# The MLP's second product by Strassen's algorithm, in seven passes over all inner features

## The chip, the cores and the metric

The kernel runs on one core of a Trainium2 chip. The metric is the device time in microseconds (us) of one execution; the time of a kernel is the median of several runs.

## The reference

A trunk of two layers over 1024 tokens of 1024 features, in float32. Each layer is a mixer with its residual and then an MLP with its residual; the mixer of layer 0 is two groups of heads ("ab"), that of layer 1 a latent attention ("MLA"). A last norm ends it. The change is in the MLP's second product:

```
for layer in range(DEPTH):
    x = x + (ab_mixer if layer % 2 == 0 else mla_mixer)(rms_norm(x, ...))
    hf = rms_norm(x, ffn_norm[layer])
    x = x + jnp.square(jax.nn.relu(hf @ ffn_w1[layer])) @ ffn_w2[layer]
return rms_norm(x, final_norm)
```

`ffn_w1` is 1024 x 4096 and `ffn_w2` 4096 x 1024.

## The kernel before

Activations lie with features on partitions: eight tiles x[m] of 128 features by 1024 tokens. To keep float32 precision each operand is split in a high and a low half of TensorE's faster type (`split`, L350, for activations, `fetch`, L255, for weights: ScalarE casts the high half, VectorE or POOL subtracts for the low one), and every product is three: high by high, high by low, low by high. Weight tiles of 512 KB come through SP's DMA queue in the order of a list written by `plan` (L230).

**First product** (`strassen_up`, L566). It goes by Strassen's algorithm in Winograd's form: 16 quads of two hidden tiles, seven products each, 12 matmuls of 128x512 a product. The order on TensorE, VectorE and ScalarE is as the code is written (a manual schedule). While product g runs, VectorE and ScalarE make the halves of the weights of product g + 3, from sums that VectorE forms (L143), and take results out of PSUM (L615 to L630). The finished hidden tiles, after relu, norm and square, go to DRAM (hd).

**Second product** (`ffn`, L446). Blocks fb of four hidden tiles; for each, four weight tiles; for each of these two output tiles; for each a `gemm` (L284) of 4 hidden tiles x 3 x 2 token halves = 24 matmuls of 128x512. So 8 x 4 x 2 x 24 = 1536 matmuls a layer. After each gemm VectorE adds 128x1024 from PSUM to x[m] (L486). The hidden tiles of the next block are loaded and split during a block (L360, L361). In layer 0 the last block calls `finish` (`next_norm`, L693) for each tile as it is done: halves for MLA, its square added to ss by VectorE (L373), and the tile stored. In layer 1 the last block goes by token pieces of 512, 256 and 256 (`f2_pieces`, L512), and `tail` (L778) does the final norm for each piece: squares, sums over features on TensorE (L381), an inverse root in a dozen small VectorE operations (L333), a spread to all partitions (L433, L435), and eight multiplications with stores (L799, L800), six on VectorE and two on POOL, stores by SP's and ScalarE's queues.

After layer 0 MLA begins with two tiles of its input projection (`latent`, L1345), 48 matmuls each, and after the tenth step of six matmuls the sums over ss (`x_col`).

Of the kernel before, what the change touches and what calls it, by code (L numbers as in the profile page):

```python
# [17 lines left out]
P = 128  # L18
D = 1024
# [4 lines left out]
FB = 8  # L24
FT = 4
# [64 lines left out]
NQ = FB * FT // 2  # L90
H5 = 512

# [80 lines left out]

class Kern:
# [55 lines left out]
    def plan(self):  # L230
        A = self.A
        w = [(A["w_g"], NK * 48, True)]
# [12 lines left out]
        self.wready = deque()  # L245

    def ffn_plan(self, layer):

        out = [None, None]
        for i in range(FB):  # L250
            for j in range(NK // 2):
                out.append((self.A["w2"][layer, i, j], 1024, layer == 1 and i == FB - 1))
        return out
# [30 lines left out]
    def gemm(self, ps, hi, lo, off, step, xh, xl, m=P, cols=FULL, ks=None):  # L284
        nc = self.nc
        n = len(xh)
        for k in range(n) if ks is None else ks:
            wh = hi[:, off + k * step:off + k * step + m]
            wl = lo[:, off + k * step:off + k * step + m]
            for i, (w, x) in enumerate(((wh, xh[k]), (wh, xl[k]), (wl, xh[k]))):  # L290
                for o, t, c in cols:
                    nc.tensor.matmul(ps[:m, o:o + c], lhsT=w, rhs=x[:, t:t + c],  # L292
                                     start=k == 0 and i == 0, stop=k == n - 1 and i == 2)
# [84 lines left out]
    def rstd_sums(self, ps, ss, nt=NC):  # L378
# [4 lines left out]
        self.drop(ss)  # L383
# [17 lines left out]
    def rstd_col(self, ss, n, name, mul=None, nt=NC):  # L401
        ps = self.bank()
        self.rstd_sums(ps, ss, nt)
        return self.rstd_from(ps, n, name, mul, nt)
# [41 lines left out]
    def ffn(self, layer, X, ss, spill, finish, pieces=None):  # L446
        nc = self.nc
        self.lo_engine = nc.vector
        hd = [self.dp.tile([P, T], F32, name=f"hd{layer}_{i}") for i in range(FB * FT)]
        hs = {}  # L450

        def load(i, t=None):
            if t is None:
                t = self.slot(name="h")
                nc.sync.dma_start(out=t, in_=hd[i])
            hs[i] = self.split(t)
            self.drop(t)

        self.strassen_up(layer, X, ss, hd, load)
        with ExitStack() as st:  # L460
            self.pairs_of_banks()
            p2 = st.enter_context(self.tc.tile_pool(name=f"pf{layer}", bufs=2, space=PSUM, reuse_waits="tile"))
            self.bank = lambda: self.pm.tile([P, 512], F32, tag="mm", name=self.uid("bank"))
            turn = [0]

            def ps_tile():
                n = turn[0]
                turn[0] += 1
                if n % 2 == 0:
                    return self.mm()  # L470
                return p2.tile([P, T], F32, tag="mm2", name=self.uid("mmb"))

            x = []

            def operands(fb):
                return [hs[fb * FT + i][0] for i in range(FT)], [hs[fb * FT + i][1] for i in range(FT)]

            def f2(fb):
                hh, hl = operands(fb)
                for mp in range(NK // 2):  # L480
                    hi, lo = self.weights()
                    for j in range(2):
                        m = 2 * mp + j
                        ps = ps_tile()
                        self.gemm(ps, hi, lo, j * 512, P, hh, hl)
                        nc.vector.tensor_tensor(out=x[m], in0=x[m], in1=ps, op=ALU.add)  # L486
                        if fb == FB - 1:
                            finish(x, m)
                    self.release()


            def f2_pieces(fb):
                hh, hl = operands(fb)
                w = []
                with self.tc.manual_schedule(engines={mybir.EngineType.PE}):
                    for pi, (t, n) in enumerate(pieces):
                        cols = slice(t, t + n)
                        for ms in ([0, 1, 2, 3], [4], [5], [6], [7]) if pi == 0 else [[m] for m in range(NK)]:

                            ps = {}  # L500
                            for ks in (range(FT - 1), (FT - 1,)):
                                for m in ms:
                                    if pi == 0 and m % 2 == 0 and ks[0] == 0:
                                        w.append(self.weights())
                                        if m < 4:
                                            self.fetch()
                                    if ks[0] == 0:
                                        ps[m] = ps_tile()
                                    self.gemm(ps[m], *w[m // 2], (m % 2) * 512, P, hh, hl, cols=((0, t, n),), ks=ks)
                            for m in ms:  # L510
                                with self.tc.high_priority():
                                    nc.vector.tensor_tensor(out=x[m][:, cols], in0=x[m][:, cols],  # L512
                                                            in1=ps[m][:, :n], op=ALU.add)
                                finish(x, m, pi)
                    self.flush()
                for p in w:
                    self.drop(*p)

            for m in range(NK):
                t = self.slot(name="x")  # L520
                nc.sync.dma_start(out=t, in_=spill[m])
                x.append(t)
            for fb in range(FB):
                if fb + 1 < FB:
                    for i in range((fb + 1) * FT, (fb + 2) * FT):
                        load(i)
                if fb == FB - 1 and pieces:
                    f2_pieces(fb)
                else:
                    f2(fb)  # L530
                for k in range(FT):
                    self.drop(*hs.pop(fb * FT + k))
# [33 lines left out]
    def strassen_up(self, layer, X, ss, hd, load):  # L566
# [10 lines left out]
        ht = deque()  # L577
# [61 lines left out]
        def square(q, i):  # L639
            c = quads[q].pop(f"c{i}")  # L640
            nc.scalar.activation(c, c, AF.Square)
            nc.sync.dma_start(out=hd[2 * q + i], in_=c)
            self.drop(c)

        with tc.manual_schedule(engines={mybir.EngineType.PE, mybir.EngineType.DVE, mybir.EngineType.Activation}):
            up.load(1)

            for g in range(4):
                product(g, range(NK // 2 - 1), last=False)
            for g in range(N):  # L650
# [5 lines left out]
                if g == 3:  # L656
                    ps = self.bank()
                    self.rstd_sums(ps, ss["ss"])
                if g == 6:
# [17 lines left out]
                if q == NQ - 1:  # L677
                    if s == 1:
                        for i in range(FT):
                            t = self.slot(name="h")  # L680
                            nc.sync.dma_start(out=t, in_=hd[i])
                            ht.append(t)
                    if 2 <= s <= 5:
                        load(s - 2, ht.popleft())
                    if s == 5:
                        self.fetch()
                evacuate(g)
            square(NQ - 1, 1)
            self.fetch()
        self.drop(rb[0])  # L690


    def next_norm(self, goff, xh, xl, state, spill):  # L693
        def finish(x, m):
            hi, lo = self.split(x[m], g=self.cst[:, goff + m:goff + m + 1])
            xh.append(hi)
            xl.append(lo)
            state["ss"] = self.sq_add(state.get("ss"), x[m])
# [40 lines left out]
    def run(self):  # L739
# [32 lines left out]
        nh, nl, st = [], [], {}  # L772
        self.ffn(0, X, s, spill[0], self.next_norm(C_CN, nh, nl, st, spill[1]))
        X, s = self.mla(nh, nl, st["ss"], spill[1], spill[2])
        self.tail(X, s, spill[2])


    def tail(self, X, s, spill):  # L778
        nc = self.nc
        pieces = ((0, 512), (512, 256), (768, 256))  # L780
        ss = [None] * len(pieces)
        rc = {}

        def finish(x, m, pi):
            t, n = pieces[pi]
            cols = slice(t, t + n)
            ss[pi] = self.sq_add(ss[pi], x[m][:, cols], n)
            nc.scalar.activation(x[m][:, cols], x[m][:, cols], AF.Copy, scale=self.cst[:, C_FIN + m:C_FIN + m + 1])
            if m < NK - 1:
                return  # L790

            def col():
                rc[pi] = self.rstd_col(ss[pi], D, f"rf{pi}", nt=n // P)

            def norm():
                rb = self.spread(rc[pi], nt=n // P, parts=False)
                for k in range(NK):
                    eng = nc.gpsimd if k % 4 == 3 else nc.vector
                    eng.tensor_tensor(out=x[k][:, cols], in0=x[k][:, cols], in1=rb[:, :n], op=ALU.mult)  # L799
                    (nc.sync if k % 2 == 0 else nc.scalar).dma_start(out=self.out[k][:, cols], in_=x[k][:, cols])  # L800
                self.drop(rb)
            self.later(10, col)
            self.later(14, norm)
        self.ffn(1, X, s, spill, finish, pieces=pieces)
# [978 lines left out]
```

## Time and profile before

| | |
|---|---|
| median of 3 runs | 2547.54 us (2546.87 to 2549.79) |
| the profiled execution | 2546.84 us, its span 2544.8 us |
| first MLP, first product | 470 to 792 us |
| first MLP, second product | 792 to 1147 us |
| second MLP, first product | 1880 to 2169 us |
| second MLP, second product | 2169 to 2526 us |
| TensorE / VectorE / ScalarE / POOL busy | 98% / 64% / 42% / 20% of the span |

The span goes from the first to the last instruction of one execution that the profiler recorded. A group's row gives engine, operation, output and inputs, shape and count, then its busy time and the mean of one in ns, and after the second bar the idle time of the engine before it with what ended that.

### The profile page before, as it was taken

How to read it: one execution, taken by the hardware profiler on the slowest of the kernel's cores; microseconds unless marked ns; L12 is line 12 of the kernel's file. 1: busy time of each engine (PE TensorE's matmuls, PEld its weight loads, DVE VectorE, ACT ScalarE, POOL GpSimd, SP SyncE). 2: the span in 40 equal slices, each digit the busy share in tenths (PEclk: the TensorE clock that was granted, in tenths of full speed). 3: DMA queues.
4: the chain of work that ended last, by engine and by line, in shares of the span. 5: the costliest groups of instructions: out<-in, count | busy, mean ns of one | idle time of the engine just before them, and what ended most of it. 6: DMA issues, size and time to landing. Idle time of an engine off the chain costs nothing.

```text
span 2544.8 us, 31331 instructions
## 1 busy us (share of the span) xinstructions
PE 2482.7 (98%) x12235; PEld 2060.7 (81%) x12235; DVE 1625.9 (64%) x2372; ACT 1066.7 (42%) x1629; POOL 520.1 (20%) x333
## 2 busy tenths in 40 slices
PE   7999989999999999999999999999999999999997
PEld 5788877788888888888788888887878888888886
DVE  6765487766667443354788888886776666634336
ACT  3354444433334111034567777776533333411113
POOL 3233244100000000003445454545300000000001
PEclk9999999999999999999999999999999999999999
DMA  3112123332336322131000000012332334622111
GB/s 113 67 58 73 36 65 107 115 116 91 123 126 248 115 76 75 50 124 51 25 18 22 18 22 17 21 51 75 129 116 99 115 110 157 231 83 99 56 53 67
DMA packets 63091, 217.20 MB, mean 85 GB/s; under 512 B 7168, under 2 KB 10176, under 8 KB 62944
## 3 DMA queue, kind: packets, MB, share of 16 engines
q1 hardware_dynamic: 60608, 210.96, 23.4%
q10 hardware_dynamic: 2304, 4.20, 0.4%
q8 instruction: 97, 1.59, 0.3%
q14 instruction: 50, 0.41, 0.1%
q0 software_dynamic: 32, 0.05, 0.0%
HBM read 160.81 MB, written 54.36 MB: 85 GB/s over the span
## 4 chain that ended last, share of the span: by engine, by line
PE 90%; DVE 7%; issue 1%; ACT 1%; DMA 0%; POOL 0%; DVEq 0%; ACTq 0%; POOLq 0%
PE mm L292 31%; PE mmb L292 14%; PE A L594 7%; PE C L594 7%; PE D L594 7%; PE s L1532 6%; PE po L1585 4%; PE pt L1566 4%; PE pj L292 4%; PE B L594 3%; DVE mx L1536 1%; PE mm L307 1%; PE intra L1213 1%; DVE nm L1538 0%; PE int L1202 0%
## 5 line engine op out<-in xcount | busy, mean ns | idle before, releaser
L292 PE MATMUL mm<-hi,wlo 128*128 128x512 f32 x1160 | 367.1, 396 | 2.6 <-POOL wlo L272 2.5
L292 PE MATMUL mm<-lo,whi 128*128 128x512 f32 x1160 | 367.7, 396 | 0.0
L292 PE MATMUL mm<-hi,whi 128*128 128x512 f32 x1160 | 367.5, 396 | 0.0
L271 ACT CAST whi<-raw 128x1024 fp32r<-128x1024 f32 (+1 forms) x117 | 121.0, 1034 | 436.4 <-PE mmb L292 318.8
L292 PEld LDWEIGHTS mm<-hi,wlo 128*128 128x128 f32 x1160 | 217.9, 189 | 52.6 <-POOL wlo L272 3.0
L292 PEld LDWEIGHTS mm<-lo,whi 128*128 128x128 f32 x1160 | 218.3, 189 | 49.0
L292 PEld LDWEIGHTS mm<-hi,whi 128*128 128x128 f32 x1160 | 218.3, 189 | 48.9 <-issue 0.6
L1551 POOL TENSOR_SCALAR pr<-pr,rs 128x1024 f32<-128x1024 f32 x128 | 143.8, 1124 | 237.9 <-DVE rs L1550 195.9
L594 PE MATMUL A<-xo,wo 128*128 128x512 f32 x768 | 190.9, 397 | 1.4 <-DVE x L719 1.4
L272 POOL TENSOR_TENSOR wlo<-raw,whi 128x1024 fp32r<-128x1024 f32 (+1 forms) x53 | 131.2, 2476 | 290.7 <-ACT whi L271 275.2
L594 PE MATMUL C<-xo,wo 128*128 128x512 f32 x768 | 188.5, 393 | 0.0
L594 PE MATMUL D<-xo,wo 128*128 128x512 f32 x768 | 188.1, 393 | 0.0
L1536 DVE TENSOR_REDUCE mx<-s 128x1 f32<-128x1024 f32 x128 | 155.6, 1215 | 44.8 <-PE s L1532 43.9
L486 DVE TENSOR_TENSOR x<-x,mmb 128x1024 f32<-128x1024 f32 x60 | 73.2, 1219 | 170.9 <-PE mmb L292 170.9
L1544 ACT ACTIVATE pr<-s,nm,rqs 128x1024 f32<-128x1024 f32 x128 | 154.6, 1208 | 52.0 <-DVE nm L1538 48.7
L594 PEld LDWEIGHTS A<-xo,wo 128*128 128x128 f32 x768 | 146.2, 191 | 35.4 <-issue 1.8
L594 PEld LDWEIGHTS C<-xo,wo 128*128 128x128 f32 x768 | 144.1, 188 | 33.7
L594 PEld LDWEIGHTS D<-xo,wo 128*128 128x128 f32 x768 | 144.2, 188 | 33.4
L1568 ACT CAST pth<-pt 128x512 fp32r<-128x512 f32 x256 | 138.0, 589 | 77.0 <-PE pt L1566 76.4
L1570 DVE TENSOR_TENSOR ptl<-pt,pth 128x512 fp32r<-128x512 f32 x256 | 163.7, 680 | 7.1 <-ACT pth L1568 6.2
L486 DVE TENSOR_TENSOR x<-x,mm 128x1024 f32<-128x1024 f32 x60 | 73.2, 1219 | 136.5 <-PE mm L292 136.5
L292 PE MATMUL mmb<-lo,whi 128*128 128x512 f32 x480 | 149.8, 393 | 0.0
(336 smaller groups left out, 4769.0 us busy)
## 6 DMA issues: line engine op xcount, KB each, us to landing
raw<-w SPq DMA_DIRECT2D x128, 512.0 KB, 3.3
hd<-c SPq DMA_DIRECT2D x64, 512.0 KB, 2.6
h<-hd SPq DMA_DIRECT2D x64, 512.0 KB, 4.6
raw<-w_in SPq DMA_DIRECT2D x24, 512.0 KB, 3.2
xs<-x SPq DMA_DIRECT2D x24, 512.0 KB, 2.6
x<-xs SPq DMA_DIRECT2D x24, 512.0 KB, 5.1
x<-xT SPq DMA_DIRECT2D x12, 512.0 KB, 6.3
Dm<-nMd SPq DMA_DIRECT2D x8, 512.0 KB, 3.4
```

The lines of the kernel that those rows point to most:

```text
L271: nc.scalar.copy(out=hi[:, :cols], in_=raw[:, :cols])
L272: self.lo_engine.tensor_tensor(out=lo[:, :cols], in0=raw[:, :cols], in1=f(hi[:, :cols]), op=ALU.subtract)
L292: nc.tensor.matmul(ps[:m, o:o + c], lhsT=w, rhs=x[:, t:t + c], start=k == 0 and i == 0, stop=k == n - 1 and i == 2)
L486: nc.vector.tensor_tensor(out=x[m], in0=x[m], in1=ps, op=ALU.add)
L594: nc.tensor.matmul(ps, lhsT=a, rhs=x, start=first and kk == 0 and j == 0, stop=last and kk == NK // 2 - 1 and j == 2, skip_group_check=not ...
L1532: nc.tensor.matmul(ps[:, hsl], lhsT=lhs[:, qs], rhs=rhs[:, hsl], start=a, stop=z)
L1536: nc.vector.reduce_max(out=mx, in_=ps, axis=AX.X)
L1544: nc.scalar.activation(pr, ps, AF.Exp, bias=nm, scale=r["qs"][:, qb:qb + 1], accum_out=su)
L1551: nc.gpsimd.tensor_scalar(out=pr, in0=pr, scalar1=rs, scalar2=1.0, op0=ALU.mult, op1=ALU.mult)
L1566: nc.tensor.transpose(pt[:, j * P:(j + 1) * P], pr[:, c * P:(c + 1) * P], self.ident)
L1568: nc.scalar.copy(out=pth[half][:, :, qo], in_=pvs[half])
L1570: nc.vector.tensor_tensor(out=ptl[half][:, :, qo], in0=pv, in1=f(pth[half][:, :, qo]), op=ALU.subtract)
```

## The change

The second product goes by Strassen's algorithm too (`strassen_down`). The output's two halves of features by two halves of tokens are the four blocks; inner features are cut in eight blocks kp. Seven passes, in the order `DOWN`, each go over all eight kp, so a pass is 8 steps of 24 matmuls of 128x512, 56 steps and 1344 matmuls a layer. The four PSUM banks of a pass collect over all eight steps, and some over two passes, and are added to x only afterwards, 40 additions of 128x512 a layer (L773), one or two a step during the next pass.

- Weights: three of the seven operands are quarters of w2, the other four are sums of quarters. The sums are made once per layer during the first product (`DownSums`, L240): for every kp four loads, four VectorE operations of 128x1024, four stores to a DRAM tensor sd. In the second product each step fetches and splits one 512 KB weight tile (56 a layer, 32 before).
- Hidden features: `DownInputs` loads quarters of 128 x (2 x 512) with rows of 2 KB, two tiles at a time, in four of the seven passes, four steps ahead; combines two quarters with one VectorE operation in four passes, three steps ahead (L199); and splits one a step, two steps ahead (56 a layer, 32 before).
- Layer 0's end: tiles 4 to 7 of x are finished during the last pass, tiles 0 to 3 after it. The squares are added to ss by POOL. MLA's first two tiles start with input tiles 4 to 7 of both, and go on with 0 to 3.
- Layer 1's end (`Tail`): tokens 512 to 1023 are complete after the last pass but one. Their squares are added by POOL in pass 4, steps 0 to 3, their sums and spread come in steps 5 and 6, and in step 7 POOL multiplies eight tiles of 128x512, each followed by a store in SP's queue. The last pass is done for tokens 0 to 255 first, with weights and inputs kept, then for 256 to 511 tile pair by tile pair; the last piece is multiplied by VectorE (six) and POOL (two).

VectorE in the second product of layer 0. Before, lo is the low half of a hidden tile h, wlo that of a weight tile, x<-x,mm the addition from PSUM:

```order
L361 TENSOR_TENSOR lo_6758<-h_6755,hi_6757 128x1024
L486 TENSOR_TENSOR x_5965<-x_5965,mm_6261 128x1024
L486 TENSOR_TENSOR x_5967<-x_5967,mmb_6287 128x1024
L272 TENSOR_TENSOR wlo_6315<-raw_6313,whi_6314 128x1024
L486 TENSOR_TENSOR x_5969<-x_5969,mm_6319 128x1024
L486 TENSOR_TENSOR x_5971<-x_5971,mmb_6345 128x1024
```

The same engine after the change, two steps of the pass that follows pass 5; hq is a hidden quarter, z a bank of pass 5:

```order
L773 TENSOR_TENSOR x_6109<-x_6109,z_6390 128x512
L773 TENSOR_TENSOR x_6111<-x_6111,z_6390 128x512
L199 TENSOR_TENSOR hq_6003<-hq_6681,hq_6003 128x1024
L412 TENSOR_TENSOR wlo_6729<-raw_6727,whi_6728 128x1024
L502 TENSOR_TENSOR lo_6760<-hq_6003,hi_6759 128x1024
L773 TENSOR_TENSOR x_6149<-x_6149,z_6391 128x512
L773 TENSOR_TENSOR x_6151<-x_6151,z_6391 128x512
L199 TENSOR_TENSOR hq_6107<-hq_6718,hq_6107 128x1024
L412 TENSOR_TENSOR wlo_6768<-raw_6766,whi_6767 128x1024
L502 TENSOR_TENSOR lo_6799<-hq_6107,hi_6798 128x1024
```

Every 24 matmuls there stand one wlo, one lo, one combination and two half additions, where there was one full addition, half a wlo and half a lo.

TensorE at the start of MLA, before: the last matmuls ahead of the sums over ss are of the second tile (mm_8144), with the first two inputs:

```order
L292 MATMUL mm_8083<-hi_8054,wlo_7990 128x512 x2
L292 MATMUL mm_8144<-hi_7799,whi_8063 128x512 x2
L292 MATMUL mm_8144<-lo_7800,whi_8063 128x512 x2
L292 MATMUL mm_8144<-hi_7799,wlo_8064 128x512 x2
L292 MATMUL mm_8144<-hi_7832,whi_8063 128x512 x2
L292 MATMUL mm_8144<-lo_7833,whi_8063 128x512 x2
L292 MATMUL mm_8144<-hi_7832,wlo_8064 128x512 x2
L381 MATMUL pt_8157<-ones,ss_7803 128x2 x8
```

And now; hi_8092 is of input tile 7, hi_8170 and hi_8178 of tiles 0 and 1, ss_7970 the sum of squares:

```order
L432 MATMUL mm_8223<-hi_8092,wlo_8162 128x512 x2
L432 MATMUL mm_8222<-hi_8170,whi_8131 128x512 x2
L432 MATMUL mm_8222<-lo_8171,whi_8131 128x512 x2
L432 MATMUL mm_8222<-hi_8170,wlo_8132 128x512 x2
L432 MATMUL mm_8222<-hi_8178,whi_8131 128x512 x2
L432 MATMUL mm_8222<-lo_8179,whi_8131 128x512 x2
L432 MATMUL mm_8222<-hi_8178,wlo_8132 128x512 x2
L522 MATMUL pt_8284<-ones,ss_7970 128x2 x8
```

The sums stay behind sixty matmuls; what is ahead of them are both tiles' second halves and two inputs of the first tile.

SP's queue at the end of layer 1, before: the last loads of weights, and the stores of the first piece:

```order
L270 DMA raw_19849<-w 128x1024
L270 DMA raw_19857<-w 128x1024
L270 DMA raw_19883<-w 128x1024
L800 DMA out<-x_18047 128x512
L800 DMA out<-x_18051 128x512
```

And now, where out<-x are the eight stores of tokens 512 to 1023, and raw_20292 is the weight tile of step 53 (the sixth of the last pass):

```order
L410 DMA raw_20215<-w 128x1024
L290 DMA out<-x_18434 128x512
L290 DMA out<-x_18316 128x512
L410 DMA raw_20253<-w 128x1024
L290 DMA out<-x_18356 128x512
L290 DMA out<-x_18396 128x512
L290 DMA out<-x_18436 128x512
L410 DMA raw_20292<-w 128x1024
L410 DMA raw_20330<-w 128x1024
L410 DMA raw_20368<-w 128x1024
```

Stores that wait for POOL's multiplications stand now among weight loads, the eighth of them ahead of the last three.

The core of the diff:

```diff
+NKP = 8
+DOWN = (1, 5, 6, 7, 3, 4, 2)
...
+class DownSums:
+    def step(self, g):
+        q, s = divmod(g, 7)
+        kp, odd = divmod(q, 2)
...
+        at = {(0, 2): 0, (0, 5): 2, (1, 1): 1, (1, 2): 3}.get((odd, s))
+        if at is not None:
...
+            v.tensor_tensor(out=o, in0=a, in1=b, op=op)
+            k.nc.sync.dma_start(out=self.sd[kp][at], in_=o)
...
+        elif (odd, s) == (1, 5):
+            self.load(kp + 1)
...
+class Tail:
+    def step(self, i, kp):
+        pool = self.k.nc.gpsimd
+        if i == 4:
+            if kp < NK // 2:
+                for m in (kp, kp + NK // 2):
+                    self.square(m, H5, H5, pool)
+            elif kp == 5:
+                self.sums(H5, H5)
+            elif kp == 6:
+                self.spread(H5, H5)
+            elif kp == 7:
+                self.out(H5, H5)
+        elif i == 2 and 2 <= kp < 2 + NK // 2:
+            self.square(kp - 2 + NK // 2, 0, H5, pool)
...
+    def strassen_down(self, layer, di, spill, finish):
...
+            for n in range(steps):
+                pi, kp = divmod(n, NKP)
+                i = DOWN[pi]
...
+                self.fetch()
+                w, o = self.weights(), di.ops[n]
...
+                    products(n, w, o, z, new)
...
+                di.load(n + 4)
...
+                di.parts(n + 2)
+                if pi > 0 and kp < NP:
+                    evacuate(DOWN[pi - 1], kp)
+                di.combine(n + 3)
+                if last:
+                    tail.step(i, kp)
+                elif i == 2 and 2 <= kp < 2 + NP:
+                    finish(x, kp - 2 + NP)
+            if not last:
+                self.fetch()
+                for p in range(NP):
+                    evacuate(2, p)
+                for p in range(NP):
+                    finish(x, p)
...
     def next_norm(self, goff, xh, xl, state, spill):
...
-            state["ss"] = self.sq_add(state.get("ss"), x[m])
+            state["ss"] = self.sq_add(state.get("ss"), x[m], eng=self.nc.gpsimd)
...
         def latent(n, goff):
...
+                early = [(self.mm(), self.weights()) for _ in range(n)]
+                for ps, w in early:
+                    self.gemm(ps, *w, 0, P, xh, xl, ks=range(NK // 2, NK), first=NK // 2, last=-1)
```

More of the change, by code (lines that the diff above doesn't have):

```diff
@@ L23 @@
 AH = 4
-FB = 8
-FT = 4
+FT = 32
 CH = 16
@@ L231, in plan @@
         A = self.A
+        self.sd = [[self.dp.tile([4, P, 1024], F32, name=f"sd{i}_{j}") for j in range(NKP)] for i in range(2)]
         w = [(A["w_g"], NK * 48, True)]
@@ L249, in ffn_plan @@
         out = [None, None]
-        for i in range(FB):
-            for j in range(NK // 2):
-                out.append((self.A["w2"][layer, i, j], 1024, layer == 1 and i == FB - 1))
+        for i in DOWN:
+            for kp in range(NKP):
+                src = self.A["w2"][layer, kp, {1: 0, 2: 2, 4: 3}[i]] if i in (1, 2, 4) else \
+                    self.sd[layer][kp][{5: 0, 6: 1, 7: 2, 3: 3}[i]]
+                out.append((src, 1024, layer == 1 and i == 2 and kp < NKP - 2))
         return out
@@ L280, in release, with gemm @@
         self.fetch()
-    def gemm(self, ps, hi, lo, off, step, xh, xl, m=P, cols=FULL, ks=None):
+    def gemm(self, ps, hi, lo, off, step, xh, xl, m=P, cols=FULL, ks=None, first=0, last=None):
         nc = self.nc
@@ L292, in gemm @@
                     nc.tensor.matmul(ps[:m, o:o + c], lhsT=w, rhs=x[:, t:t + c],
-                                     start=k == 0 and i == 0, stop=k == n - 1 and i == 2)
+                                     start=k == first and i == 0,
+                                     stop=k == (n - 1 if last is None else last) and i == 2)
             self.tick()
@@ L440, in spread @@
         return self.spread_sums(self.spread_parts(col, nt, parts), nt, parts)
[L446 to L532, printed above, removed]
@@ L535, in part, with ffn @@
+    def ffn(self, layer, X, ss, spill, finish=None):
+        self.lo_engine = self.nc.vector
+        hd = [self.dp.tile([4, P, T], F32, name=f"hd{layer}_{i}") for i in range(NKP)]
+        di = DownInputs(self, hd)
+        self.strassen_up(layer, X, ss, hd, di)
+        self.strassen_down(layer, di, spill, finish)
+        self.pairs_of_banks()
     def part(self, src, o):
@@ L563, in strassen_inputs, with strassen_up @@
         self.drop(u, v)
-    def strassen_up(self, layer, X, ss, hd, load):
+    def strassen_up(self, layer, X, ss, hd, di):
         nc, tc = self.nc, self.tc
@@ L576, in strassen_up @@
         quads = {}
-        ht = deque()
+        sums = DownSums(self, layer)
         def product(g, ks=range(NK // 2), last=True):
@@ L646, in strassen_up @@
             up.load(1)
+            sums.load(0)
             for g in range(4):
@@ L677, in strassen_up @@
                 if q == NQ - 1:
[L678 to L684, printed above, removed]
+                    if s < 4:
+                        di.load(s)
+                    if s in (2, 4):
+                        di.parts(s // 2 - 1)
@@ L771, in run @@
         X, s = self.ab(xh, xl, ss, spill[0])
-        nh, nl, st = [], [], {}
+        nh, nl, st = [None] * NK, [None] * NK, {}
         self.ffn(0, X, s, spill[0], self.next_norm(C_CN, nh, nl, st, spill[1]))
         X, s = self.mla(nh, nl, st["ss"], spill[1], spill[2])
[L775 to L804, printed above, removed]
+        self.ffn(1, X, s, spill[2])
     def ab(self, xh, xl, ss, spill):
@@ L1366, in latent @@
             hs, ls, ss = [], [], None
-            for m in range(n):
-                ps = self.proj(xh, xl)
+            early = []
+            if goff == C_KVG:
+                early = [(self.mm(), self.weights()) for _ in range(n)]
+                for ps, w in early:
+                    self.gemm(ps, *w, 0, P, xh, xl, ks=range(NK // 2, NK), first=NK // 2, last=-1)
+            for m in range(n):
+                if early:
+                    ps, w = early[m]
+                    self.gemm(ps, *w, 0, P, xh, xl, ks=range(NK // 2), first=-1, last=NK // 2 - 1)
+                    self.release()
+                else:
+                    ps = self.proj(xh, xl)
                 hi, lo = self.split(ps, g=self.cst[:, goff + m:goff + m + 1])
```

174 lines of the change are left out of this document (166 added, 8 removed).

## The prediction

> **What bounds the kernel now.** I read the page first, its busy table and the chain that ended last, then the windows by stage, then the pieces of the chain inside the stages that the change touches, and the groups by line for durations. The page's busy row of TensorE and its chain by engine:
>
> ```profile
> PE 2482.7 (98%) x12235; PEld 2060.7 (81%) x12235; DVE 1625.9 (64%) x2372; ACT 1066.7 (42%) x1629; POOL 520.1 (20%) x333
> PE 90%; DVE 7%; issue 1%; ACT 1%; DMA 0%; POOL 0%; DVEq 0%; ACTq 0%; POOLq 0%
> ```
>
> The windows are the first MLP's two products (first 470 to 792, second to 1147), the second MLP's (1880 to 2169, to 2480), its piecewise end, and the tail. Columns: length, then PE, PEld, DVE, ACT and POOL busy, granted clock, DMA share, GB/s.
>
> ```profile
> 470.00:792.00 322.00, 320.41 (x1385) 259.62 (x1384) 220.35 (x316) 125.58 (x188) 2.94 (x2) 0.99 0.35 126
> 792.00:1147.00 355.00, 355.00 (x1538) 288.58 (x1538) 162.98 (x140) 78.73 (x77) 1.90 (x2) 1.00 0.30 104
> 1880.00:2169.00 289.00, 289.00 (x1253) 235.09 (x1252) 193.63 (x269) 112.17 (x167) 0.00 (x0) 1.00 0.36 127
> 2169.00:2480.00 311.00, 311.00 (x1349) 253.03 (x1348) 137.02 (x118) 61.86 (x61) 0.00 (x0) 1.00 0.28 99
> 2480.00:2525.00 45.00, 42.83 (x266) 37.91 (x265) 28.93 (x69) 20.93 (x41) 3.50 (x2) 1.00 0.13 47
> 2525.00:2545.00 20.00, 6.76 (x43) 5.70 (x41) 12.17 (x35) 4.04 (x10) 3.69 (x4) 0.69 0.31 106
> ```
>
> In every MLP stage but the last 20 us TensorE is busy without a gap, at full clock, and nobody else is near the limit. So the time of these stages is the number of matmuls times their spacing. The chain's pieces give the spacing:
>
> ```profile
> 508.47 2.79 PE D L594 x12
> 1141.00 5.51 PE mmb L292 x24
> 2524.85 1.42 PE mmb L292 x12
> ```
>
> A 128x512 matmul takes 5.51/24 = 0.230 in the second product and 2.79/12 = 0.2325 in the first, which is already by Strassen with one weight tile to every matmul; I take 0.231. A 128x256 one takes 1.42/12 = 0.118.
>
> **The change part by part.**
>
> *Matmuls.* The second product goes from 8 x 4 x 2 x 24 = 1536 matmuls of 128x512 a layer to 7 passes x 8 steps x 24 = 1344. 192 x 0.231 = 44.4 us a layer, 88.7 in both: the whole gain. The Trainium skill ("TensorE: Matmul & The Clock Gate", Back-to-back issue gap) has 512/2.4 + 2.5 = 216 ns for such a matmul; by it the gain would be 82.9 us. The trace has 0.231, and that decides.
>
> *VectorE in the second product.* A step of 24 matmuls now lasts 5.55 us. In it VectorE makes the low half of a weight tile, the low half of an input, up to two 128x512 additions, and in four of the seven passes a combination of two hidden quarters.
>
> ```profile
> L272 DVE TENSOR_TENSOR wlo<-raw,whi 128x1024 fp32r<-128x1024 f32 x62 | 75.6, 1219 | 4.0 <-ACT whi L271 4.0
> L361 DVE TENSOR_TENSOR lo<-h,hi 128x1024 fp32r<-128x1024 f32 x64 | 76.2, 1220 | 53.3 <-ACT hi L360 52.9 <-DMA x<-xs 0.3
> L143 DVE TENSOR_TENSOR s<-raw,s 128x512 f32<-128x512 f32 x32 | 21.9, 684 | 0.0
> L360 ACT CAST hi<-h 128x1024 fp32r<-128x1024 f32 x32 | 32.9, 1048 | 78.4 <-DMA h<-hd 77.0 <-DMA hd<-c 1.3
> ```
>
> The worst step is 3 x 1.22 + 2 x 0.69 = 5.04 of 5.55 us, in 4 of 8 steps after pass 5; the others are 3.7 to 4.4. ScalarE has 2 x 1.05. It fits, with 0.5 us to spare, and operands are made two steps ahead: cost 0. If it did not fit, every step would carry the excess (a rival below).
>
> *VectorE in the first product.* The sums of w2 quarters add 4 x 8 = 32 operations of 1.22 = 39 us a layer, and 64 transfers of 512 KB. VectorE goes from 220 to 259 of 322 us. Its idle time there is waiting for ScalarE's cast of its own next operand:
>
> ```profile
> L538 DVE TENSOR_TENSOR wo<-s,wo 128x512 fp32r<-128x512 f32 x127 | 87.2, 688 | 83.2 <-ACT wo L537 82.7
> L538 DVE TENSOR_TENSOR wo<-raw,wo 128x512 fp32r<-128x512 f32 x95 | 65.3, 688 | 45.5 <-ACT wo L537 45.3
> ```
>
> That is 128 us over the 32 quads of both layers, 4.0 a quad (7 products, 7 x 2.79 = 19.5 us). The four sums of two quads are 4.9 us and fall into 8.0 us of such waits, and weights are prepared three products ahead. Cost 0. Traffic goes from 126 to about 126 + 33.5 MB/322 us = 230 GB/s, and the start of the trace shows what the queues can carry:
>
> ```profile
> 5.00:10.00 5.00, 1.06 (x2) 0.23 (x2) 2.21 (x2) 3.11 (x4) 3.98 (x3) 1.00 1.03 419
> raw<-w SPq DMA_DIRECT2D x128, 512.0 KB, 3.3
> h<-hd SPq DMA_DIRECT2D x64, 512.0 KB, 4.6
> ```
>
> The sums are loaded 9 or more products (25 us) before use, against 3.3 to land. Cost 0. In the second product a step loads at most 1 MB, 1.05/5.55 = 189 GB/s.
>
> *The end of layer 0.* After the last pass x[0..3] get their last addition, are split for MLA and squared; the square sums are now added by POOL, not VectorE. MLA's first two tiles start with inputs 4 to 7. The chain as it is there now, then groups by line:
>
> ```profile
> 1146.51 13.84 PE mm L292 x60
> 1160.36 1.68 PE pt L381 x16
> ```
> ```profile
> L373 POOL TENSOR_TENSOR ss<-ss,sq 128x1024 f32<-128x1024 f32 x14 | 34.6, 2470 | 47.3 <-ACT sq L372 47.2
> L357 DVE SCALAR_TENSOR_TENSOR lo<-x,cst,hi 128x1024 fp32r<-128x1024 f32 x8 | 10.3, 1284 | 5.2 <-ACT hi L356 4.9
> L356 ACT ACTIVATE hi<-x,cst 128x1024 fp32r<-128x1024 f32 x8 | 9.2, 1153 | 18.6 <-DVE x L486 18.6
> L372 ACT ACTIVATE sq<-x 128x1024 f32<-128x1024 f32 x8 | 8.3, 1043 | 0.0
> ```
>
> The sums over ss stay behind 60 matmuls, so TensorE reaches them 60 x 0.231 = 13.9 us after the pass (T). VectorE first finishes a weight tile whose buffer the last step frees (1.05 on ScalarE, 1.22), so the four additions end at T + 2.3 + 4 x 0.69 = 5.05. ScalarE then does hi and square by turns from T + 3.0, four times 2.2: the last square ends at T + 11.8, and one POOL addition of 2.47 later is T + 14.3: stall 0.4. But POOL's additions and VectorE's four lo's (1.28) hold one another up. Timeline of POOL and of VectorE where both had two SBUF operands:
>
> ```profile
> 409.42 2.40 POOL L272 TENSOR_TENSOR wlo<-raw,whi 128x1024 fp32r<-128x1024 f32 x1 [1.28 <-ACT whi L271]
> ```
> ```profile
> 409.89 2.48 DVE L538 TENSOR_TENSOR xo<-y,xo 128x512 fp32r<-128x512 f32 x1 [0.47 <-ACT xo L537]
> ```
>
> The VectorE operation took 2.48, against 0.68 for such an operation in the L143 row above: it ended 0.55 after POOL's. So from the first square (T + 5.2) four pairs of 2.47 + 1.28 in full alternation end at T + 20.2: stall 6.3. Some lo's lie in POOL's waits for squares; nearer the serial end I take 4.
>
> *The clock after a stall.* In the tail TensorE is idle for most of 2529 to 2532, and then the granted clock falls; the third row is from the start of the program:
>
> ```profile
> 2529.00:2532.00 3.00, 0.53 (x5) 0.33 (x3) 2.76 (x8) 0.96 (x3) 0.05 (x1) 1.00 0.82 280
> 2532.00:2535.00 3.00, 1.01 (x4) 0.93 (x4) 1.64 (x9) 0.58 (x2) 0.00 (x0) 0.57 0.08 27
> 15.00:20.00 5.00, 1.10 (x3) 0.20 (x1) 5.00 (x2) 5.00 (x6) 4.90 (x3) 1.00 0.44 179
> ```
>
> But in 15 to 20, with TensorE idle for 3.9 of 5 us, it stayed at 1.00. A stall of 4 us may or may not drop it; I add 0 and keep 2 us (4 us of work at half clock) for the range. The Trainium skill ("TensorE: Matmul & The Clock Gate", What's actually happening) says that an idle window of 3.4 us halves the clock until a busy one has passed. By that rule the stall costs about 1.7 us more; the second of these rows agrees with it, the third does not.
>
> *Layer 1's last pass and tail.* Forty-eight steps take 48 x 24 x 0.231 = 266.1. Pass 2 runs in two token halves of 256 columns: 384 x 0.118 = 45.3. While its first half runs (8 steps of 2.84 us), POOL multiplies the finished half of the output (8 operations of 128x512), starting some 4 us before the pass (what they multiply by leaves TensorE at the end of the last step but one, 5.55 us before, and is copied by ScalarE), and SP's queue holds the remaining weight loads behind the output stores, each of which waits for its multiplication. Half of the 2.47 row is 1.24; contending with VectorE's 1.22 it is 2.46 each. So the eighth multiplication ends 4 us before + 9.9 = 5.9, or + 19.7 = 15.7 us, into the pass. Three weight loads follow it; the first is needed by step 53, 5 x 2.84 = 14.2 us in, and takes 3.3 + 1.05 + 1.22 = 5.6 from issue to use. Stall 0 to 7.1; VectorE has ten such operations in that time, so near the upper end: 6. The sums and spreads between pieces cost TensorE about 2.8 (two of sums like the 1.02 below, two of spreads like the 0.45). The end is one piece of 256 tokens as before; from the chain's pieces:
>
> ```profile
> 2526.27 0.45 PE bank L433 x2
> ...
> 2532.01 0.43 DVE ss L373
> ...
> 2532.49 1.02 PE bank L381 x4
> ```
>
> From 2532.45 to the span's end are 12.35 us, which stay. After the last matmul one addition, one square and one sum of about 0.43 come first: 13.7, say 14. Before, the last matmul ended 15.3 before the end of the span:
>
> ```profile
> 2529.25 0.28 PE L292 MATMUL mmb<-hi,klo 128*128 128x256 f32 x1
> ```
>
> There multiplications of an earlier piece stood in VectorE's way.
>
> *Sum.* Layer 0: -44.4 + 4 = -40.4. Layer 1 from 2169.2: 266.1 + 45.3 + 6 + 2.8 + 14 = 334.2, against 375.6: -41.4. Together -81.8. The profiled execution is 2546.84, with a span of 2544.8; 2546.84 - 81.8 = 2465.0. It lies 0.7 below the median of the runs, so 2465.7, say **2466**.
>
> **The rivals.**
>
> *No stalls (12%).* The lo's and multiplications fall into each other's gaps: both stalls go, 2466 - 10 = 2456. For: POOL was often waiting in the rows above. Against: the two rows at 409.
>
> *VectorE binds in part (18%).* In the first product it is at 80%, in the second at up to 91%. If half of the 39 us of sums a layer delays a product, that is 39 us: 2505; if steps with a combination take 5.85 instead of 5.55, 64 x 0.3 = 19 us: 2485. Against: TensorE never waits for the operand split in the first product's window now (320.4 of 322 busy). If all sums lay on the path, 78 us: 2544, no change (2%).
>
> *Loads one after the other: slower (4%).* In passes 1, 5, 6 and 4 each step needs a weight load and a hidden load, in rows of 2 KB and through one queue. If these go one behind the other, 3.3 + 4.6 = 7.9 us, 2.35 over a step: 64 steps x 2.35 = 150 us, 2616. It is slower than before from 5.55 + 81.8/64 = 6.83 us a pair. Against: 419 GB/s in the row above is 1 MB in 2.5 us, so transfers overlap.
>
> That the change does less than it says: the counts of matmuls stand in the program, so I give that nothing of its own.
>
> **How the numbers follow.** My forecast (2458 to 2475) has 64%. The range takes in the case without stalls, the serial ends of both (2466 + 3.4 + 2) and the lower part of the VectorE rival: 2453 to 2490. A measurement of this kernel can tell about 0.2%, 5 us, from no change. Faster is the forecast, no stalls and the VectorE rival, 64 + 12 + 18 = 94%; same 2%; slower 4%.
>
> **What would show it.** Right: TensorE without gaps in the passes, 24 matmuls in 5.5 us; the second product of layer 0 about 310 us long; a wait of a few us for POOL's ss at its end; another in layer 1's last pass for a weight's low half, behind stores in SP's queue; 14 us from the last matmul to the end. Wrong: waits for VectorE or for hidden quarters at every step, a first product longer than 322 us, or a total off 2466 by more than the stalls.

## The result, and the profile after

The changed kernel takes 2483.3 us (median of 4 runs, 2480.6 to 2486.1), the one before 2548.7; the ratio is 0.974 (95% interval 0.972 to 0.976). 2466 was forecast, 2453 to 2490 given. The profiled execution has a span of 2482.6 us against 2544.8: 62 us less, where the sum of the prediction had 82. The busy row and the chain of the page:

```profile
PE 2405.1 (97%) x11947; PEld 1999.9 (81%) x11947; DVE 1773.4 (71%) x2504; ACT 1159.5 (47%) x1717; POOL 576.3 (23%) x362
PE 87%; DVE 7%; DMA 3%; ACT 1%; issue 1%; POOL 1%; DVEq 0%; ACTq 0%; POOLq 0%; SPq 0%
```

The windows of the changed kernel, cut at its own stages (columns as in the prediction): first MLP's first and second product; its end to MLA's first scores; from these to the second MLP; its first product; its passes up to the last; the last pass's first half, its second half, and the end.

```profile
473.60:794.20 320.60, 317.08 (x1365) 256.62 (x1364) 248.27 (x340) 123.84 (x185) 2.50 (x1) 0.99 0.62 224
794.20:1105.80 311.60, 310.55 (x1346) 252.04 (x1345) 197.87 (x184) 117.75 (x119) 11.23 (x5) 1.00 0.47 159
1105.80:1198.00 92.20, 87.56 (x408) 72.58 (x406) 47.70 (x75) 39.92 (x44) 39.54 (x18) 0.94 0.18 61
1198.00:1827.30 629.30, 609.72 (x3701) 528.08 (x3699) 504.63 (x820) 417.98 (x702) 305.24 (x219) 0.99 0.12 41
1827.30:2147.20 319.90, 316.10 (x1364) 255.98 (x1365) 246.89 (x338) 123.84 (x185) 2.52 (x1) 0.99 0.62 223
2147.20:2416.70 269.50, 268.06 (x1163) 217.21 (x1162) 174.36 (x176) 107.92 (x115) 14.27 (x10) 1.00 0.46 156
2416.70:2445.50 28.80, 24.46 (x193) 23.00 (x193) 24.96 (x19) 16.23 (x20) 17.76 (x9) 1.00 0.48 163
2445.50:2469.20 23.70, 23.67 (x200) 23.41 (x198) 7.84 (x26) 6.38 (x15) 5.15 (x8) 1.00 0.08 28
2469.20:2482.60 13.40, 1.77 (x6) 1.02 (x6) 6.37 (x21) 1.30 (x3) 2.46 (x3) 0.69 0.32 108
```

The second product of layer 0 has 1344 matmuls in 311.6 us (354.9 before): 43.4 us gained of 44.4. Layer 1's, to the end, takes 335.4 us (375.8 before), where 334.2 were forecast. These two are nearly the forecast. What is missing lies in the other stages. The same stages in the profile of before took 317.5 us (first product, now 320.6), 83.7 (to the first scores, now 92.2, of which 4 were forecast), 622.2 (to the second MLP, now 629.3) and 316.6 (now 320.0). Added up, these are 18.1 us more than forecast, and the two second products 2.2: that is the 20. TensorE's waits, longest first, help to find where:

```profile
PE pt L1714 <- DVE ptl L1718: 12.5, 13, 2.9
...
PE B L574 <- DVE dg L561: 7.3, 4, 3.2
...
PE pt L522 <- POOL ss L514: 4.2, 1, 4.2
PE y L792 <- DVE klo L412: 3.8, 4, 1.4
```

Four places, then: ptl in MLA, whose program is the old one (10.1 us in the profile of before), dg, mainly in the two first products (3.2 before), ss at the end of layer 0, and the low halves klo of the last pass. Waits add up to less than the loss, since the clock falls behind some of them. The windows behind the wait for ss:

```profile
1120.00:1124.00 4.00, 0.06 (x1) 0.06 (x1) 1.69 (x1) 0.00 (x0) 3.81 (x2) 0.81 0.00 0
1124.00:1128.00 4.00, 4.00 (x18) 3.90 (x19) 0.38 (x3) 0.00 (x0) 0.00 (x0) 0.50 0.00 0
1128.00:1132.00 4.00, 4.00 (x11) 3.13 (x10) 3.63 (x14) 0.00 (x0) 0.00 (x0) 0.50 0.00 0
1132.00:1136.00 4.00, 4.00 (x17) 3.18 (x17) 1.89 (x2) 2.50 (x3) 2.75 (x2) 0.91 0.00 0
```

After 4 us without work TensorE runs for over 8 us at half its clock: busy, in the profile's words, and yet half as fast. The 92.2 us are 8.5 longer than before, 4.2 of it the wait and 4.3 the clock.

### The profile page after: what moved, and what is told of

Same layout as the page of the kernel before. It is cut to its first block, busy times and chain, and to the rows that moved or that the text cites. A ratio compares the mean times of both kernels' runs of the same rounds, so it can differ in the third digit from the quotient of the medians.

```text
span 2482.6 us, 31418 instructions
## 1 busy us (share of the span) xinstructions
PE 2405.1 (97%) x11947; PEld 1999.9 (81%) x11947; DVE 1773.4 (71%) x2504; ACT 1159.5 (47%) x1717; POOL 576.3 (23%) x362
## 4 chain that ended last, share of the span: by engine, by line
PE 87%; DVE 7%; DMA 3%; ACT 1%; issue 1%; POOL 1%; DVEq 0%; ACTq 0%; POOLq 0%; SPq 0%
PE mm L432 18%; PE y L792 11%; PE z L792 11%; PE A L655 7%; PE C L655 6%; PE D L655 6%; PE s L1680 6%; PE po L1733 4%; PE pt L1714 4%; PE pj L432 4%; PE B L655 3%; DMA raw<-w 1%; DVE mx L1684 1%; DMA hq<-hd 1%; DVE nm L1686 1%
## 5 line engine op out<-in xcount | busy, mean ns | idle before, releaser
L411 ACT CAST whi<-raw 128x1024 fp32r<-128x1024 f32 x163 | 169.2, 1038 | 453.1 <-issue 226.5
L412 DVE TENSOR_TENSOR wlo<-raw,whi 128x1024 fp32r<-128x1024 f32 x110 | 138.6, 1260 | 208.9 <-ACT whi L411 204.8
L432 PE MATMUL mm<-hi,wlo 128*128 128x512 f32 x680 | 218.1, 399 | 2.6 <-POOL wlo L412 2.5
L432 PE MATMUL mm<-hi,whi 128*128 128x512 f32 x680 | 218.4, 399 | 0.0
L432 PE MATMUL mm<-lo,whi 128*128 128x512 f32 x680 | 218.3, 399 | 0.0
L792 PE MATMUL y<-hi,wlo 128*128 128x512 f32 (+1 forms) x464 | 180.7, 389 | 2.5 <-DVE wlo L412 2.5
L792 PE MATMUL y<-hi,whi 128*128 128x512 f32 (+1 forms) x464 | 180.8, 390 | 0.0
L792 PE MATMUL y<-lo,whi 128*128 128x512 f32 (+1 forms) x464 | 180.3, 389 | 0.0
L792 PE MATMUL z<-hi,whi 128*128 128x512 f32 (+1 forms) x400 | 155.9, 390 | 0.0
L792 PE MATMUL z<-hi,wlo 128*128 128x512 f32 (+1 forms) x400 | 155.1, 388 | 0.5 <-DVE wlo L412 0.5
```

What stands on the lines that cost most here:

```text
L411: nc.scalar.copy(out=hi[:, :cols], in_=raw[:, :cols])
L412: self.lo_engine.tensor_tensor(out=lo[:, :cols], in0=raw[:, :cols], in1=f(hi[:, :cols]), op=ALU.subtract)
L792: nc.tensor.matmul(Z[z, p][:, :c], lhsT=l[:, m], rhs=r[:, k], start=new and kp == 0 and kk == 0 and j == 0, stop=kp == NKP - 1 and kk == 1 ...
```

## The experiments

The theory to be tested: the change brings 43 to 44 us in each layer by its matmuls, and gives back about 20 us more than was reckoned with in these places, each with a cause of its own. The rivals: a general cost of the change (VectorE near its limit, doubled traffic), or an effect of the clock that has nothing to do with the waits. Stage times below are from the profile of each kernel, in the same cuts.

**ss on VectorE** (e1).

```diff
-            state["ss"] = self.sq_add(state.get("ss"), x[m], eng=self.nc.gpsimd)
+            state["ss"] = self.sq_add(state.get("ss"), x[m])
```

> The square sums at layer 0's end go back from POOL to VectorE. Theory (POOL and VectorE hold one another up there, and the stall halves TensorE's clock for some 9 us): the wait of 4.2 us for ss and the slow matmuls behind it (another 4.4 us) both go, from the end of layer 0's second product to the first attention scores 84 us instead of 92; 8 to 9 us less in all. Rival (the low clock has nothing to do with the stall): only the wait goes, 4 us less. Rival (VectorE is then late itself): a stall of over 1 us for ss stays.

2478.0 us, 5.3 less: between the theory and the first rival. From the end of the second product to the first scores there are 85.7 us instead of 92.2. The wait is gone; of the clock's part some 2 us stay. The chain of this kernel shows VectorE's work, one square behind the other, ending just ahead of the sums, and its windows a shorter dip of the clock:

```profile
1117.20 1.23 DVE ss L514
...
1118.47 1.95 PE pt L522 x16
```
```profile
1118.40:1121.00 2.60, 2.54 (x20) 2.44 (x20) 0.49 (x4) 0.00 (x0) 0.00 (x0) 1.00 0.00 0
1121.00:1124.00 3.00, 3.00 (x8) 2.32 (x8) 2.63 (x13) 0.00 (x0) 0.00 (x0) 0.50 0.00 0
```

Sixteen matmuls of two columns lie between, 1.95 us, and no gap of 0.1 us is in the profile there. These seem to be enough for half a clock behind them, but no run tests that: the profile of e10 below, with the same edit, has the same dip (0.53 in the 3.4 us behind them), the one of before has the same sixteen matmuls and a clock of 1.00. So the wait costs its own 4.2 us and 2.3 us of the clock; 2 us of the clock stay without it.

**Sums later** (e2).

```diff
+        if kp == 0:
+            ats = {(1, 1): (0, 2), (1, 2): (1,), (1, 3): (3,)}.get((odd, s), ())
```

> The weight sums of the first kp are moved out of the first quad, so that none stands ahead of the spread of the norm (dg) on VectorE; all others stay. Theory (two sums in the first quad delay dg, TensorE waits 3.2 instead of 1.0 us and runs at a lower clock behind it): 3 us less in each layer's first product, 318 instead of 320.6 us each; 5 to 6 us less in all. Rival (the longer first product comes from more VectorE work or traffic over all quads): no change.

2472.9 us. The first products take 317.5 and 316.1 us, which are the old kernel's 317.5 and 316.6 to half a microsecond, with all 64 weight sums still made and their 128 transfers still added. So the sums and their traffic cost nothing where they stand beside matmuls, and 3.1 and 3.8 us a layer where two of them stand ahead of dg, about 2 us of each for the longer wait and the rest for the clock behind it. The chain of the changed kernel, pieces between 484 and 500:

```profile
486.61 1.22 DVE w2q L240
...
495.06 1.14 DVE w2q L240
496.19 0.60 DVE c L685
...
497.07 2.28 DVE dg L561 x2
...
499.39 0.79 PE B L574
```

The two w2q take 2.4 us ahead of dg, and the wait grew from 1.0 to 3.2. The whole kernel gained 10 us, more than the 7 of these stages and than the 5 to 6 expected; the rest is in MLA (625.3 us), below.

**The last pass.** Its first half takes 28.8 us from its first matmul, where 192 x 0.118 = 22.7 are needed. (The 34 us in two expectations were counted from the last wait ahead of it, in the step before.) Its VectorE, in the timeline of the changed kernel:

```profile
2416.66 2.31 DVE L412 TENSOR_TENSOR klo<-raw,khi 128x1024 fp32r<-128x1024 f32 x1
2418.89 2.33 DVE L502 TENSOR_TENSOR lo<-hq,hi 128x1024 fp32r<-128x1024 f32 x1
2421.14 0.67 DVE L773 TENSOR_TENSOR x<-x,z 128x512 f32<-128x512 f32 x1
2421.74 1.71 DVE L412 TENSOR_TENSOR klo<-raw,khi 128x1024 fp32r<-128x1024 f32 x1
```

Operations of 1.22 take up to 2.3 while POOL multiplies; that from PSUM takes its 0.67. The chain there goes from a low half to the load that takes over its raw tile, and SP's queue waited for klo before five of its weight loads:

```profile
2416.66 2.32 DVE klo L412
...
2418.99 4.30 DMA raw<-w
```
```profile
SPq L410 <- DVE klo L412: 5.9, 5, 2.3
```

The stores between these loads waited 13.7 us for POOL in all, but in the queue's timeline each load still waits for a VectorE operation, klo or lo, when the stores ahead of it are out. So a late klo delays TensorE twice, itself and through a later weight tile. Stores to ScalarE's queue (e3), as the edit in `out` and a call after the last step:

```diff
+            if a == H5:
+                continue
...
+                    if i == 2 and kp == 7:
+                        tail.store()
```

> The eight stores of tokens 512 to 1023 are issued by ScalarE's queue after its last weight cast; POOL multiplies as before. Theory A (the weight loads behind the stores in SP's queue set the pace of the last pass's first half): that half takes 23 to 25 us instead of 34, 9 us less. Theory B (the shared port of POOL and VectorE sets it: 16 operations of VectorE at 2.3 instead of 1.2 us): it stays above 30 us, at most 3 us less. Both together: between.

2482.7 us, first half 29.0: no gain. The low halves still take up to 2.3 us, TensorE waits 4.8 us for them (3.8 before this edit), and the loads, with no store ahead of them now, still wait for klo:

```profile
SPq L417 <- DVE klo L419: 25.0, 6, 4.9
```

So it is theory B: the stores in SP's queue are not what holds the pass. Multiplications on VectorE (e4):

```diff
-            eng = nc.vector if both and m % 4 != 3 else nc.gpsimd
+            eng = nc.vector if a == H5 or both and m % 4 != 3 else nc.gpsimd
```

> The eight multiplications of tokens 512 to 1023 go from POOL to VectorE (4.9 us by 0.6 each), stores stay in SP's queue. By theory A (queue) and B (port) alike the last pass's first half falls from 34 to 23 to 26 us, 8 to 11 us less, since VectorE's operations take 1.2 again and the stores wait for nothing long. Rival (the pass is bound by its own work of casts, low halves and loads at 2.84 us a step): it stays above 30 us.

2481.3 us, first half 27.6: hardly more, where 23 to 26 was expected by either theory. In this kernel klo and lo take 1.22 again, but the eight multiplications, 4.9 us, now stand on VectorE ahead of a klo for which TensorE waits 1.43 us, and the weight tile that takes over its raw tile comes late. The chain there, then ScalarE's wait for that tile, which makes TensorE wait 0.81 us, then the window, in which the DMA engines are busy for 98%:

```profile
2413.60 2.21 DVE x L289 x4
...
2416.01 1.89 DVE x L289 x3
2417.90 1.15 DVE klo L412
...
2419.06 4.47 DMA raw<-w
```

```profile
2423.61 1.05 ACT L411 CAST khi<-raw 128x1024 fp32r<-128x1024 f32 x1 [5.77 <-DMA raw<-w]
```
```profile
2414.00:2420.00 6.00, 4.57 (x36) 4.29 (x35) 6.00 (x9) 2.00 (x2) 0.00 (x0) 1.00 0.98 374
```

So this edit moved the stall from POOL to VectorE's own order. The next takes multiplications and stores away from the half altogether, by a later spread, on which both depend (e6), and one more takes the squares out too (e7; its edit is not shown):

```diff
-            elif kp == 6:
-                self.spread(H5, H5)
-            elif kp == 7:
-                self.out(H5, H5)
...
+                    if p == 0:
+                        tail.spread(H5, H5)
+                        tail.out(H5, H5)
```

> The spread, multiplications and stores of tokens 512 to 1023 come after the last pass's first half, so neither POOL's multiplications nor their stores run beside it; squares stay there. The half takes 28.7 us now. If multiplications and queue were all: 23 us. If ScalarE's casts and squares (3.2 us a step in four steps, against 2.84 of TensorE) remain as a third limit: 25 us. If low halves alone set it: over 28. The end after the last matmul stays at 13.4 us.

> As with the late spread, and the squares of tiles 4 to 7 (tokens 0 to 511) also come after the first half, added by VectorE. Theory (ScalarE is the third limit): the first half falls to 23 us, 2 less than with the late spread alone; the second half stays below 25 us. Rival: no further gain, or the second half grows by as much.

2479.4 and 2480.4 us. The first half takes 22.7 us in both: full speed. ScalarE is no third limit, and the squares cost nothing. The eight multiplications hold the pass: on POOL they slow VectorE's low halves, on VectorE they stand ahead of them, and only without them beside it does it run. What the traffic of the stores adds in e4 was not separated. The second half grew from 23.7 to 26.0 us: it now has the spread's own matmuls (0.87 us), and TensorE waits there 1.2 us for a dg of the next piece, while POOL multiplies.

**MLA** (e5). The changed kernel has an execution of 629.3 us there, others of the same code between 625.3 and 629.5, the old one 622.2. In the timeline of the changed kernel, on VectorE and on POOL:

```profile
1709.18 1.23 DVE L1684 TENSOR_REDUCE mx<-s 128x1 f32<-128x1024 f32 x1 [0.53 <-PE s L1680]
1710.44 3.52 DVE L1686 TENSOR_TENSOR nm<-mx,rqn 128x1 f32<-128x1 f32 x1
```
```profile
1708.11 2.42 POOL L502 TENSOR_TENSOR lo<-ord,hi 128x1024 fp32r<-128x1024 f32 x1
1710.49 1.15 POOL L1699 TENSOR_SCALAR pr<-pr,rs 128x1024 f32<-128x1024 f32 x1
1711.58 2.38 POOL L502 TENSOR_TENSOR lo<-ord,hi 128x1024 fp32r<-128x1024 f32 x1
```

A product of one column, which takes 0.16 us in most of its 128 instances, starts in the last moment of a POOL operation and ends when two more of POOL's have ended. TensorE waits 2.9 us for what follows, and its clock falls. One edit gives the product only one tensor operand:

```diff
-            nc.vector.tensor_tensor(out=nm, in0=mx, in1=r["qn"][:, qb:qb + 1], op=ALU.mult)
+            nc.vector.tensor_scalar(out=nm, in0=mx, scalar1=r["qn"][:, qb:qb + 1], scalar2=None, op0=ALU.mult)
```

> In MLA's softmax the 128x1 product nm = mx x rqn on VectorE is formed with a scalar per partition instead of a second tensor; nothing else differs. In the changed kernel's profile one such product took 3.52 us, while POOL ran two operations back to back, and a wait of 2.9 us on TensorE follows. Theory (it lost the shared port to POOL): no nm takes over 0.3 us, and from the first scores to the second MLP's first product there are 620 to 623 us instead of 625.3 to 629.4; 4 to 7 us less in all. Rival (the wait on TensorE has another cause): no change.

2473.8 us, 619.3 us in the stage: 9.5 us less in all (8.2 against the later runs of the changed kernel, e12), more than expected. The group's row of nm, changed kernel, this one, and the kernel before:

```profile
L1686 DVE TENSOR_TENSOR nm<-mx,rqn 128x1 f32<-128x1 f32 x128 | 64.8, 506 | 4.4
```
```profile
L1686 DVE TENSOR_SCALAR nm<-mx,rqn 128x1 f32<-128x1 f32 x128 | 27.4, 214 | 4.5
```
```profile
L1538 DVE TENSOR_TENSOR nm<-mx,rqn 128x1 f32<-128x1 f32 x128 | 61.4, 480 | 4.4
```

Is that a loss of the change, or of the old kernel too? The same edit in the kernel before (e11), and the changed kernel once more (e12):

> The kernel before, with nm formed with one tensor operand. Its profile has no nm over 1.9 us and 622.2 us from the first scores to the second MLP's first product. Theory (the port is lost now and then in this kernel too, and more often by chance of alignment in the changed one): about 619 us there, 2 to 4 us less in all, so a third of what it brings in the changed kernel. Rival (what the changed kernel loses there is in the old one as well): 7 to 10 us less.

> The changed kernel once more, beside the two others. Theory (the held nm at the end of MLA comes with this program's alignment, not by chance of a run): again an nm of 3 us or more some 516 us after the first scores, and 625 to 630 us from there to the first product of the second MLP; 2480 to 2486 us. Rival (chance of the run): an execution without it, 622 us there.

The kernel before with this edit takes 2543.3 us, 0.997 of the one without (0.996 to 0.998). Beside it that one takes 2552.9 us, so the edit brings 9.6 us there (6 to 11 by the interval): the rival's 7 to 10, and not a third. The stages say less: 617.7 us, 4.5 less than in the profile of before, which at 2546.84 us is one of that kernel's shorter executions (2544.6 to 2554.9). The expectation also misread that profile: it has three nm of 2.27 to 2.30 us. So by the medians most of what the edit brings was to be had in the old kernel too, and how much of it the change had lost is open.

The changed kernel again: 2482.0 us, again an nm of 3.53 us, 512 us after the first scores, and 626.0 us in the stage. An nm of 3.0 us or more is in every profile of the changed kernel and its variants in which nm has two operands (after, e1 to e4, e6 to e8, e12), and not in the one profile of before. So it comes with the program, as far as one profile of before can tell. Why the changed program, with the same order of instructions there, meets POOL in that moment and the old one does not was not tried.

The 3.3 us between the two profiles of the changed kernel are the clock: TensorE's waits in the stage are the same, but the first has two dips and the second none. The first, then the second, behind the held nm and 17 us later:

```profile
1715.00:1720.00 5.00, 4.96 (x26) 4.63 (x27) 3.30 (x7) 2.73 (x6) 2.25 (x2) 0.66 0.07 5
1732.00:1737.00 5.00, 4.60 (x17) 3.75 (x18) 2.20 (x5) 2.53 (x5) 2.91 (x2) 0.66 0.01 2
```
```profile
1713.00:1718.00 5.00, 4.93 (x33) 4.45 (x34) 3.33 (x7) 3.13 (x7) 2.25 (x2) 1.00 0.22 62
1730.00:1735.00 5.00, 5.00 (x30) 4.34 (x29) 1.29 (x2) 1.64 (x3) 3.15 (x2) 1.00 0.00 2
```

Two times 5 us at 0.66 cost 3.4 us. Why the same wait is followed by a dip in one execution and not in another is open. Of the 7.1 us that this stage lost in the first profile, these are 3.4; the other 3.6 are TensorE's waits for ptl and for pr, 14.8 us instead of 11.2. With nm from one tensor operand these waits are 8.4 us in the changed kernel (e5) and 8.9 in the old one (e11), so that difference was nm's.

**VectorE's margin** (e8). In layer 0's second product, per step:

```diff
+                if not last:
+                    nc.vector.tensor_tensor(out=scr, in0=f(w[0]), in1=f(w[1]), op=ALU.add)
```

> In layer 0's second product every step gets one more VectorE operation of 128x1024 (1.22 us, its result unused), 56 in all. Theory (a step leaves VectorE over 1 us on average, and operands two steps ahead even out the fuller ones): the second product stays at 311.6 to 313 us. Rival (VectorE at 5.04 of 5.55 us is at its edge): the full steps of three passes take 6.26 us, and the product grows by 9 to 20 us.

2507.7 us; the product takes 335.4 us instead of 311.6. The theory fell: 24 us of the 68 us of added work came onto the path. Nearly the same stretch of the changed kernel and of this one:

```profile
798.00:1105.00 307.00, 305.94 (x1326) 248.31 (x1325) 194.30 (x181) 117.13 (x117) 11.23 (x5) 1.00 0.47 156
```
```profile
798.00:1130.00 332.00, 317.19 (x1331) 245.99 (x1330) 261.89 (x237) 117.04 (x117) 10.20 (x5) 1.00 0.43 143
```

VectorE is busy for 79% there, 63% in the changed kernel. TensorE waits 9.6 us for wlo and 4.1 us for whi, where it waited 1.1 us for wlo; VectorE itself still waits 69.6 us for casts. So the added work does not hide, but VectorE is not simply full. One doubt stays: the added operation reads the weight tile of its step, and so may also free its buffer later; the two were not separated.

**All mended** (e10): the edits of e1, e2, e5 and e6, the last with its eight multiplications on VectorE.

> Four edits together: square sums of layer 0's end on VectorE, the first weight sums out of the first quad, nm with one tensor operand, and the spread of tokens 512 to 1023 after the last pass's first half, with its multiplications on VectorE. If their effects add up, by stages against the changed kernel: -6.5 (layer 0 to MLA's scores), -3 and -4 (first products), -10 (MLA), -6 in the last pass's first half and at most +1.5 in its second: 28 us less, 2455 us (2450 to 2460). Rival (one stall hides another): over 2462.

2454.5 us, 0.962 of the kernel before (0.961 to 0.964), and 27.5 us less than the changed kernel beside it. Its stages: 317.5, 311.5, 85.6, 618.7, 316.1, 269.5, then 22.7, 24.6 and 13.6. 28 us less was forecast by adding up, and each stage moved as the single edit had moved it, to about 1 us; no stall hid another.

## Why the prediction was right in its main term and 17 us off

- *Matmuls: right.* 88.7 us forecast; 43.4 us in layer 0, and layer 1's passes nearly as reckoned (269.5 us, where 266.1 and, for the sums and the spread inside them, 1.7 come to 267.8). 0.231 us a matmul held (311.6/1344 = 0.232). The 0.216 of the Trainium skill ("TensorE: Matmul & The Clock Gate", Back-to-back issue gap), which that section gives for the isolated gap and not for a stream of matmuls with their weights, would have been 6 us short.
- *VectorE in the second product, cost 0: right, by little.* 311.6 us against 310.5. The full steps of 5.04 us are eight and not four: the additions of pass 6 meet combinations too, in pass 7. That there is little room above 5.04 of 5.55 us fits e8, where one operation more a step cost 24 us, with the doubt said there.
- *VectorE in the first product, cost 0: wrong.* This step failed by 6.4 us. The argument was an average: 4.9 us of sums in 8.0 us of waits per two quads. It holds in all other quads, as e2 shows, and not in the first, where VectorE carries the norm's dozen small operations and dg, for which TensorE waits. The rival's mechanism (a sum delays a product) was the right one, at one place instead of half of them.
- *The end of layer 0: the size was right.* 4 us forecast, 4.2 measured. Four POOL additions took 12.96 us, 3.2 each instead of 2.47, and three of VectorE's lo's beside them 9.82, 3.3 each instead of 1.28: the alternation is there, though not full. The 4 was chosen between 0.4 and 6.3, so some luck is in it. POOL's row and VectorE's:

```profile
1110.93 12.96 POOL L514 TENSOR_TENSOR ss<-ss,sq 128x1024 f32<-128x1024 f32 x4 [15.16 <-ACT sq L513]
```
```profile
1111.87 9.82 DVE L498 SCALAR_TENSOR_TENSOR lo<-x,cst,hi 128x1024 fp32r<-128x1024 f32 x3 [0.23 <-ACT hi L497]
```

- *The clock, cost 0: wrong.* This term was mis-sized: it is 4.3 us there, and it comes behind the wait for dg and in MLA as well (0.53 from 500 to 505, 0.66 from 1715 to 1720). The rows of the trace were read as undecided. The rule of the Trainium skill ("TensorE: Matmul & The Clock Gate", What's actually happening), by which an idle window halves the clock until at least one busy window has passed, was on the right side; the 1.7 us that the prediction worked out from it took the least, one window.
- *Layer 1's last pass and tail: right as a sum, the first part by luck.* 6 us of stall forecast, 6.1 measured (28.8 - 22.7), 14 for the end, 13.4 measured. The mechanism was told as a queue: weight loads behind stores that wait for slowed multiplications. This step was wrong: without the stores in that queue (e3) the half took 29.0 us. The runs showed that VectorE's low halves themselves take up to 2.3 us beside POOL's multiplications, and that the loads wait for these low halves.
- *What was not looked at.* MLA has no edit but its first two tiles, so its stage got no term; in its profile it lost 7.1 us, 3.4 by the clock and 3.6 by waits that e5 takes away. By the medians the kernel before gains about as much by that edit (e11), so this loss is not shown to be the change's alone.
- *Loads one after the other: did not happen.* No wait of TensorE for a hidden quarter is in the profile; at the start of the second product, with x loaded too, six weight tiles took 9.5 us to land in the median (3.3 before), and TensorE waited 0.53 us twice.

## What to carry to other kernels

A cost that is hidden on average is looked up once more at the place where the covering engine does something special: the first turn of a loop, where a norm or a spread hangs on it. A wait is to be priced with what the clock does behind it. And where an edit that should remove a stall brings nothing, read in its profile what is waited for now: the edit may have put a stall of the same length in the place of the old one, as multiplications moved to VectorE did here.

## What the runs showed that was not expected

- In two profiles (e1, e10) TensorE ran at about half its clock for some 3 us behind less than 2 us of matmuls of two columns, without a wait; in the profile of before the same matmuls had no such dip behind them.
- An operation of one column on VectorE with two operands in SBUF took up to 3.53 us while POOL ran operations back to back; with one tensor operand it took 0.21 on average, and the kernel became 8 to 10 us shorter, the changed one and the old one alike.
- The same wait of 2.9 us in MLA was followed by half a clock in one execution of the changed kernel and not in another, 3.4 us in all.
